# A feed forward block in float32: the first product by seven half-sized products, the second with half the tokens' sums held in PSUM

## The chip, the cores and the metric

The kernel runs on one core of one Trainium2 chip. The metric is the device time of one execution in microseconds (us), lower is better, here as the median of 3 runs. The core has five engines that run side by side and wait for each other by semaphores: TensorE (PE) multiplies, VectorE (DVE), ScalarE (ACT) and GpSimd (POOL) work on elements, and SyncE (SP) issues the transfers (DMA), in the order of its queue.

## The reference, cut to what matters

Two blocks are computed, one behind the other, on 1024 tokens of width 1024, all in float32. The change is in the last piece of the second block, which is

```
x = x + mix @ w_out_2                          # 1024 x 1024
h = rmsnorm(x, norm2_g_2)
x = x + square(relu(h @ w_up_2)) @ w_down_2    # 1024 -> 4096 -> 1024
return rmsnorm(x, final_g_2)
```

## The kernel before

A float32 operand is split into a high part that PE takes in its fast float32 form (F32R) and a rest: ACT copies the high part, DVE subtracts it (`split`, L248; `weights`, L252, the same). A product is then three matmuls (`mm3`, L242 to L246): high x high, high x rest, rest x high. PE adds them up in a PSUM bank of 128 x 512; there are eight banks.

Memory is laid out by hand in a few large tiles: `xa` and `xc` hold the split, transposed tokens (`xh`, `xl`) and the split weights (three slots each for high and rest, `rwh`, `rwl`), `fa` holds raw loads (`rraw`, two slots) and float32 data, and a phase tile (`self.ta`; t604a, t791a, t816a in the rows) is given out anew by `phase`. A slot is used in turn by a ring, so who writes a slot waits for the last reader of what lay there.

`block3` (L1965) does the last piece. `project` multiplies with `w_out_2` in four column groups, eight token tiles each. In the fourth group each finished tile gets its residual (L1980), its norm (square on ACT L469, the root on POOL L464, the scaling L1984 on DVE) and is transposed on PE and split (`flip`, L1374). Then the loop over f0 runs: for each pair of hidden columns f (128 wide) it loads a piece of `w_up_2`, forms the hidden values of all 1024 tokens (`gemm_t`, 2 x 24 matmuls), takes relu and square and splits them (L1999 to L2002), loads and splits a row block of `w_down_2` (L2006), and multiplies the pair with it for all eight token tiles, adding each result on DVE to x in SBUF (L2021, 256 times). The whole second block is emitted in one `tc.block(schedule_with_timeline_sim=True)`: the framework's scheduler chooses each engine's order, which then is fixed in the program. All transfers are in SP's queue.

Of the kernel before, what the change touches and what calls it, by code (L numbers as in the profile page):

```python
# [191 lines left out]
class Kernel:  # L192
    def __init__(self, tc, es, A):
        self.tc, self.nc, self.A = tc, tc.nc, A
        self.cst = self.pool(es, "cst", 1)
        self.sm = self.pool(es, "sm", 2)
        self.dr = self.pool(es, "dr", 1, space=DRAM)
        ap = self.pool(es, "ap", 1)
        pp = self.pool(es, "pp", 1, space=PSUM)
        self.xa = ap.tile([128, 22912], F32R, name="xa")  # L200
        self.fa = ap.tile([128, FO + FS], F32, name="fa")
        self.pa = pp.tile([128, 4096], F32, name="psum")
        self.uid = 0
# [4 lines left out]
        self.xc = self.pool(self.xes, "xc", 1).tile([128, 4096], F32R, name="xc")  # L208
        self.xr = [ring(self.xa, 8192 * g, 4096, 2) for g in range(2)] + [ring(self.xc, 0, 2048, 2)]
        self.rraw = ring(self.fa, 0, 1088, 2)  # L210
        self.rwh, self.rwl = ring(self.xa, 16384, 1088, 3, Slots), ring(self.xa, 19648, 1088, 3, Slots)
# [1296 lines left out]
    def conformer_out(self, ys):  # L1508
        nc, V = self.nc, self.nc.vector
        zr = ring(self.xa, 8192, 1024, 4)  # L1510
# [290 lines left out]
    def diff_attention(self, W, ys):  # L1801
# [16 lines left out]
        for i in range(len(seq) + LAG + 1):  # L1818
# [146 lines left out]
    def block3(self):  # L1965
        nc, V, A = self.nc, self.nc.vector, self.A
        self.tes.close()
        self.xes.close()
        self.phase(F32, TS + 4096)
        rx = self.F(0, 1024, 8)  # L1970
        rr = self.F(8192, 512, 2)
        self.rny = self.T(0, 1024, 3)
        g2 = self.T(3072, 1024, 1).get()
        nc.sync.dma_start(g2.ap, A["norm2_g_2"].broadcast_to([128, 1024]))
        self.pg, self.pt = self.banks(0, 1, 2, 3, 4), self.banks(5, 6, 7)
        x = [rx.get() for t in range(8)]
        for qd, _, t, p in self.project(A["w_out_2"][0], range(8), ks=K_OUT):
# [3 lines left out]
            if qd == 3:  # L1981
# [3 lines left out]
                self.flip(y, *self.xdst(t))  # L1985
        self.phase(F32R, TS + 4096)
        rhh, rhl = self.T(0, 1024, 4), self.T(4096, 1024, 4)
        rdh, rdl = self.T(8192, 1024, 3), self.T(11264, 1024, 3)
        G = 2
        for f0 in range(0, 32, G):  # L1990
            hs, ds = [], []
            for f in range(f0, f0 + G):
                w = self.weights([A["w_up_2"][0][:, f * 128:(f + 1) * 128]], 8, 128)
                hh, hl = rhh.get(), rhl.get()
                for g in range(2):
                    p = self.gemm_t(w, g, 512)
                    r = rr.get()
                    gs = slice(g * 512, g * 512 + 512)
                    nc.scalar.activation(r.ap, p.ap, AF.Relu)  # L1999
                    nc.scalar.activation(hh[:, gs], r.ap, AF.Square)  # L2000
                    V.tensor_tensor(r.ap, r.ap, r.ap, op=ALU.mult)
                    V.tensor_tensor(hl[:, gs], r.ap, hh[:, gs].bitcast(F32), op=ALU.subtract)  # L2002
                hs.append((hh, hl))
                self.done(w)
                rw = self.rraw.get([128, 1024])
                nc.sync.dma_start(rw.ap, A["w_down_2"][0][f * 128:(f + 1) * 128])  # L2006
                dh, dl = rdh.get(), rdl.get()
                self.split(dh.ap, dl.ap, rw.ap)
                ds.append((dh, dl))
            if f0 + G == 32:  # L2010
                fg = self.rraw.get([128, 1024])
                nc.sync.dma_start(fg.ap, A["final_g_2"].unsqueeze(0).broadcast_to([128, 1024]))
                self.rny = ring(self.xa, 0, 1024, 2)
            for t in range(8):
                ts = slice(t * 128, t * 128 + 128)
                for c in range(2):
                    cs = slice(c * 512, c * 512 + 512)
                    p = self.pg.get()
                    for i in range(G):
                        self.mm3(p.ap, hs[i][0][:, ts], hs[i][1][:, ts], ds[i][0][:, cs], ds[i][1][:, cs], i == 0, i == G - 1)  # L2020
                    V.tensor_tensor(x[t][:, cs], x[t][:, cs], p.ap, op=ALU.add)  # L2021
                if f0 + G == 32:
                    self.rms_row(x[t].ap, fg.ap)
                    nc.sync.dma_start(A["out"][t * 128:(t + 1) * 128], x[t].ap)
        self.tes.close()

    def run(self):
        self.mix = self.dr.tile([8, 128, NTOK], F32, name="mix")
        self.x1 = self.dr.tile([NTOK, 1024], F32, name="x1")
        self.x2 = self.dr.tile([NLAT, 1024], F32, name="x2")  # L2030
        self.x3 = self.dr.tile([NLAT, 1024], F32, name="x3")
# [43 lines left out]
```

## Time and profile before

| | us |
|---|---|
| median of 3 runs (2859.57 to 2865.55) | 2861.37 |
| the profiled execution, its time | 2860.13 |
| its span in the trace | 2858.4 |
| PE busy in it | 2705.8 (95%) |
| DVE, ACT, POOL busy | 1757.2, 1279.8, 594.0 |

Times in the rows count from the start of the span. A group of rows gives an instruction's line in the kernel, its engine, what it writes and reads, how often, and the mean length of one. A busy PE in these rows is PE with a matmul under way; its matmuls overlap, so the step from one start to the next tells the pace.

### The profile page before, as it was taken

How to read it: one execution, taken by the hardware profiler on the slowest of the kernel's cores; microseconds unless marked ns; L12 is line 12 of the kernel's file. 1: busy time of each engine (PE TensorE's matmuls, PEld its weight loads, DVE VectorE, ACT ScalarE, POOL GpSimd, SP SyncE). 2: the span in 40 equal slices, each digit the busy share in tenths (PEclk: the TensorE clock that was granted, in tenths of full speed). 3: DMA queues.
4: the chain of work that ended last, by engine and by line, in shares of the span. 5: the costliest groups of instructions: out<-in, count | busy, mean ns of one | idle time of the engine just before them, and what ended most of it. 6: DMA issues, size and time to landing. Idle time of an engine off the chain costs nothing. (4 is left out here: it accounts for less than half of the span.)

```text
span 2858.4 us, 43860 instructions
## 1 busy us (share of the span) xinstructions
PE 2705.8 (95%) x16606; PEld 2349.1 (82%) x16606; DVE 1757.2 (61%) x3684; ACT 1279.8 (45%) x2873; POOL 594.0 (21%) x760
## 2 busy tenths in 40 slices
PE   7999989999999999999998897899899999999998
PEld 3888879998889788888887786788798888888887
DVE  4788755546647787566364579788636444444445
ACT  4666545546526666456462332476523121121122
POOL 0122213413100122123130348265300000000000
PEclk9999999999999999999999999999999999999999
DMA  7001021212554111121135431432412111111111
GB/s 246 26 17 53 25 62 39 58 54 81 174 186 130 32 45 35 42 51 56 51 78 167 155 102 30 150 96 80 130 45 74 39 58 48 42 59 45 45 52 59
DMA packets 243616, 215.69 MB, mean 75 GB/s; under 512 B 14576, under 2 KB 222796, under 8 KB 243148
## 3 DMA queue, kind: packets, MB, share of 16 engines
q1 hardware_dynamic: 243404, 212.88, 24.5%
q8 instruction: 130, 2.13, 0.3%
q14 instruction: 82, 0.67, 0.1%
HBM read 178.39 MB, written 34.45 MB: 74 GB/s over the span
## 5 line engine op out<-in xcount | busy, mean ns | idle before, releaser
L244 PE MATMUL psum<-xa 128*128 128x256 f32 (+2 forms) x2992 | 1008.2, 338 | 8.9 <-ACT xa L265 1.9
L245 PE MATMUL psum<-xa 128*128 128x256 f32 (+2 forms) x2992 | 998.8, 334 | 5.9 <-POOL xa L266 3.7
L246 PE MATMUL psum<-xa 128*128 128x256 f32 (+2 forms) x2992 | 995.3, 333 | 2.9 <-POOL xa L266 2.2
L244 PEld LDWEIGHTS psum<-xa 128*128 128x128 f32 x2992 | 575.0, 193 | 61.3 <-ACT xa L265 2.9
L245 PEld LDWEIGHTS psum<-xa 128*128 128x128 f32 x2992 | 574.9, 192 | 55.2 <-POOL xa L266 3.9
L246 PEld LDWEIGHTS psum<-xa 128*128 128x128 f32 x2992 | 573.6, 192 | 51.2 <-POOL xa L266 2.8
L464 POOL TENSOR_TENSOR rsb<-rsa,half 128x1 f32<-128x1 f32 (+1 forms) x129 | 89.8, 696 | 1106.9 <-DVE rsa L462 1048.6
L266 DVE TENSOR_TENSOR xa<-fa,xa 128x1024 fp32r<-128x1024 f32 (+1 forms) x116 | 142.3, 1229 | 210.9 <-ACT xa L265 200.7
L265 ACT ACTIVATE xa<-fa 128x1024 fp32r<-128x1024 f32 (+1 forms) x136 | 143.8, 1059 | 283.1 <-PE psum L245 125.6
L2021 DVE TENSOR_TENSOR fa<-fa,psum 128x512 f32<-128x512 f32 x256 | 174.0, 686 | 126.9 <-PE psum L246 126.9
L805 POOL TENSOR_SCALAR fa<-fa,esk 128x640 f32<-128x640 f32 (+2 forms) x144 | 112.1, 791 | 449.6 <-DVE esk L803 342.9
L246 PE MATMUL psum<-t816a 128*128 128x512 f32 x512 | 199.5, 390 | 0.0
L245 PE MATMUL psum<-t816a 128*128 128x512 f32 x512 | 199.4, 389 | 0.0
L244 PE MATMUL psum<-t816a 128*128 128x512 f32 x512 | 199.3, 390 | 0.0
L249 ACT ACTIVATE t816a<-fa 128x1024 fp32r<-128x1024 f32 x32 | 34.0, 1061 | 358.7 <-PE psum L246 300.2
L1008 DVE SCALAR_TENSOR_TENSOR fa<-fa,vec 128x640 f32<-128x640 f32 (+2 forms) x128 | 110.4, 869 | 51.8 <-ACT fa L1006 43.3
L798 ACT ACTIVATE fa<-fa,nmx 128x640 f32<-128x640 f32 (+2 forms) x144 | 110.7, 769 | 34.8 <-DVE nmx L789 33.2
L789 DVE CUSTOM_DVE_ANT_0 fa<-psum,amask,nsink 128x640 f32<-128x640 f32 (+2 forms) x144 | 111.4, 773 | 21.1 <-PE psum L784 16.1
L246 PEld LDWEIGHTS psum<-t816a 128*128 128x128 f32 x512 | 96.1, 188 | 20.3
L245 PEld LDWEIGHTS psum<-t816a 128*128 128x128 f32 x512 | 96.1, 188 | 20.2
L244 PEld LDWEIGHTS psum<-t816a 128*128 128x128 f32 x512 | 96.1, 188 | 20.1
L1504 DVE SCALAR_TENSOR_TENSOR t604a<-t604a,cols 128x1024 f32<-128x1024 f32 x60 | 105.7, 1765 | 2.5 <-ACT t604a L1501 1.3
(472 smaller groups left out, 5148.3 us busy)
## 6 DMA issues: line engine op xcount, KB each, us to landing
fa<-in_w_in_dram SPq DMA_DIRECT2D x64, 512.0 KB
fa<-in_w_ada_dram SPq DMA_DIRECT2D x48, 512.0 KB
fa<-in_w_up_dram SPq DMA_DIRECT2D x32, 512.0 KB
fa<-in_w_down_dram SPq DMA_DIRECT2D x32, 512.0 KB
fa<-in_w_out_dram SPq DMA_DIRECT2D x24, 512.0 KB
fa<-in_w_in_dram SPq DMA_DIRECT2D x32, 256.0 KB
fa<-mix SPq DMA_DIRECT2D x18, 448.0 KB
x<-fa SPq DMA_DIRECT2D x62, 128.0 KB
```

The costliest lines, as they stand in the source:

```text
L244: mm(out, lh, rh, start=start, stop=False)
L245: mm(out, lh, rl, start=False, stop=False)
L246: mm(out, ll, rh, start=False, stop=stop)
L265: self.nc.scalar.activation(h.ap, r.ap, AF.Copy)
L266: (self.nc.gpsimd if self.wpool else self.nc.vector).tensor_tensor(l.ap, r.ap, h.ap.bitcast(F32), op=ALU.subtract)
L464: self.nc.gpsimd.tensor_tensor(r, e, self.half.broadcast_to([128, m]), op=ALU.pow)
L789: TTR = lambda o, i, m, init, acc: V.tensor_tensor_reduce(out=o, in0=i, in1=m, scale=-0.125, scalar=init, op0=ALU.add, op1=ALU.min, accum_ ...
L798: nc.scalar.activation(p[:, :nk], p[:, :nk], AF.Exp, scale=-1.0, bias=out, accum_out=sm[:, j:j + 1])
L805: nc.gpsimd.tensor_scalar(P[j][:, :nk], P[j][:, :nk], e[:, j:j + 1], 0.0, op0=ALU.mult, op1=ALU.add)
L1008: nc.vector.scalar_tensor_tensor(y, U[i][:, lo + tap:hi + tap], col(tap), y, op0=ALU.mult, op1=ALU.add)
L1504: self.nc.vector.scalar_tensor_tensor(y.ap, z[:, j:j + 1024], self.col("dw", 2 * j + i), y.ap, op0=ALU.mult, op1=ALU.add)
L2021: V.tensor_tensor(x[t][:, cs], x[t][:, cs], p.ap, op=ALU.add)
```

## The change

`w_up` is multiplied by Strassen's scheme. The 1024 tokens, the 1024 input channels and the 4096 hidden columns are cut in two halves each, and instead of eight products of half blocks there are seven (`UP`), each of a sum or difference of token blocks with a sum or difference of weight blocks. I call them product 0 to 6, and the eight column groups of 256 in each a unit: a unit has 24 matmuls of 128 x 512, so there are 56 units. The token blocks come from `z`, the transposed normalized tokens in float32 (ACT copies them from PSUM, L1990; no split there any more); POOL adds them (L2026) and they are split once for each product. A unit's weights are loaded (one or two pieces of 512 KB), added on POOL where there are two (L2042), and split. Each result goes to one or two of four accumulators: the first time by an ACT copy (L2076), later by a DVE addition (L2079). After its last contribution ACT takes relu and square in place (L2083, L2084) and SP stores it to `hd` in DRAM (L2085). `down` then takes half the tokens at a time: the sums of 512 tokens x 1024 columns stay in the eight banks over all 32 hidden groups, and hidden values and `w_down` are loaded and split for each pair of groups (L2100, L2106), `w_down` once for each half. The residual x goes by DRAM (`x4`) and comes back for one addition per bank. To make room, x stands in the phase tile until then, so its loads (L1978) move; tiles `xc` and a new `xg` are given back before the seven products.

```
-        self.xa = ap.tile([128, 22912], F32R, name="xa")
+        self.xa = ap.tile([128, 14720], F32R, name="xa")
...
+        self.xc, self.xg = xp.tile([128, 4096], F32R, name="xc"), xp.tile([128, 8192], F32R, name="xg")
+        self.xr = [ring(self.xa, 0, 4096, 2), ring(self.xg, 0, 4096, 2), ring(self.xc, 0, 2048, 2)]
...
     def block3(self):
...
-        self.phase(F32, TS + 4096)
-        rx = self.F(0, 1024, 8)
+        self.phase(F32)
+        rx, self.rny = self.T(0, 1024, 8), self.T(8192, 1024, 2)
+        z = self.F(0, 8192, 1).get([128, 8, NLAT])
...
+        self.z, self.rop, self.rtmp = z, ring(self.xa, 0, 2048, 4), self.rny
...
-                self.flip(y, *self.xdst(t))
-        for f0 in range(0, 32, G):
-            hs, ds = [], []
-            for f in range(f0, f0 + G):
-                w = self.weights([A["w_up_2"][0][:, f * 128:(f + 1) * 128]], 8, 128)
...
-            for t in range(8):
-                ts = slice(t * 128, t * 128 + 128)
+                nc.sync.dma_start(self.x4[t * 128:(t + 1) * 128], x[t].ap)
+                for i in range(2):
+                    tr = self.pt.get()
+                    for k in range(4):
+                        o = (4 * i + k) * 128
+                        nc.tensor.transpose(tr[:, k * 128:(k + 1) * 128], y[:, o:o + 128], self.ident)
+                    nc.scalar.activation(z[:, 4 * i:4 * i + 4, t * 128:(t + 1) * 128], tr.re("p (k n) -> p k n", k=4), AF.Copy)
+                if t == 6:
+                    first = list(self.up_tokens(0))[-1]
+        self.rraw.i = 0
+        raw = Ring(self.fa, [0, 1088], 1024)
+        ahead = [self.up_weights(0, 0, raw)]
+        self.tes.close()
+        self.xes.close()
+        self.phase(F32, TS + 12288)
+        raw.extend(self.T(18432, 1024, 4))
...
+    UP = [
+        ([(0, 0), (0, 1)], ALU.add, [(1, 1)], None, [((0, 0), -1), ((0, 1), 1)]),
+        ([(0, 0)], None, [(0, 1), (1, 1)], ALU.subtract, [((0, 1), 1), ((1, 1), 1)]),
+        ([(0, 0), (1, 1)], ALU.add, [(0, 0), (1, 1)], ALU.add, [((0, 0), 1), ((1, 1), 1)]),
+        ([(0, 1), (1, 1)], ALU.subtract, [(1, 0), (1, 1)], ALU.add, [((0, 0), 1)]),
+        ([(1, 1)], None, [(1, 0), (0, 0)], ALU.subtract, [((0, 0), 1), ((1, 0), 1)]),
+        ([(1, 0), (1, 1)], ALU.add, [(0, 0)], None, [((1, 0), 1), ((1, 1), -1)]),
+        ([(1, 0), (0, 0)], ALU.subtract, [(0, 0), (0, 1)], ALU.add, [((1, 1), 1)]),
+    ]
...
+    def up_tokens(self, m):
...
+            if op:
+                r = self.rtmp.get([128, 2, 512])
+                self.nc.gpsimd.tensor_tensor(r.ap, *src, op=op)
...
+    def up_weights(self, m, j, raw):
...
+        if op:
+            self.nc.gpsimd.tensor_tensor(rs[0].ap, rs[0].ap, rs[1].ap, op=op)
+        h, l = self.rwh.get([128, 4, 256]), self.rwl.get([128, 4, 256])
+        self.split(h.ap, l.ap, rs[0].ap)
...
+    def up(self, cur, raw, ahead):
...
+        cs = self.T(0, 512, 36, Slots)
...
+            for a in range(2):
+                p = self.pg.get()
+                for k in range(4):
+                    c = slice(a * 128, a * 128 + 128)
+                    self.mm3(p.ap, w[0][:, k, c], w[1][:, k, c], h[:, k], l[:, k], k == 0, k == 3)
+                f = 2 * j + a
+                for c, sign in self.UP[m][4]:
+                    if (c, f) not in acc:
+                        acc[c, f] = [cs.get(), left[c]]
+                        nc.scalar.activation(acc[c, f][0].ap, p.ap, AF.Copy, scale=float(sign))
+                    else:
+                        o = acc[c, f][0].ap
+                        V.tensor_tensor(o, o, p.ap, op=ALU.add if sign > 0 else ALU.subtract)
+                    acc[c, f][1] -= 1
+                    if not acc[c, f][1]:
+                        o = acc.pop((c, f))[0]
+                        nc.scalar.activation(o.ap, o.ap, AF.Relu)
+                        nc.scalar.activation(o.ap, o.ap, AF.Square)
+                        nc.sync.dma_start(self.hd[16 * c[1] + f, :, c[0] * 512:c[0] * 512 + 512], o.ap)
+                        cs.free(o)
...
+    def down(self, raw):
...
+        for t in range(2):
+            ps = [self.pg.get() for _ in range(8)]
+            last = []
+            for f in range(0, 32, 2):
+                o = operands(t, f)
+                if f >= 28 and t == 1:
+                    last.append(o)
+                    continue
+                for tt in range(4):
+                    for c in range(2):
+                        product(ps[2 * tt + c], o, tt, c)
```

What moves, at three places. The first is PE at the end of the last projection. Before, the products with `w_up` (128x512) begin while tiles are still being transposed (L1374):

```order
L1374 MATMUL psum<-ident,t791a 128x128 [waits DVE_49]
L1374 MATMUL psum<-ident,t791a 128x128 x3
L244 MATMUL psum<-xa 128x256
L245 MATMUL psum<-xa 128x256
L244 MATMUL psum<-xa 128x512 [waits Activation_49]
```

Now six tiles are transposed (L1989) ahead of the first 128x512 matmul, and POOL does the first half of product 0's token sum (L2026) ahead of the last two tiles' roots (L465), the second half behind them:

```order
L1989 MATMUL psum<-ident,t791a 128x128 [waits DVE_49,Activation_49]
L1989 MATMUL psum<-ident,t791a 128x128 x3
L1989 MATMUL psum<-ident,t791a 128x128 [waits Activation_49]
L1989 MATMUL psum<-ident,t791a 128x128 x3
L245 MATMUL psum<-xa 128x512 [waits Activation_49]
L245 MATMUL psum<-xa 128x512 x3
L1989 MATMUL psum<-ident,t791a 128x128 [waits DVE_49]
L1989 MATMUL psum<-ident,t791a 128x128 x7
L246 MATMUL psum<-xa 128x512 [waits DVE_49]
```

```order
L465 TENSOR_TENSOR rsb_20186<-rsa_20184,half 128x1 [waits DVE_49,Pool_49]
L2026 TENSOR_TENSOR t791a<-fa 128x1024 [waits DVE_49,DMAHW1_49,PE_49,Activation_49]
L465 TENSOR_TENSOR rsb_20230<-rsa_20228,half 128x1 [waits DVE_49,Pool_49]
L465 TENSOR_TENSOR rsb_20280<-rsa_20278,half 128x1 [waits DVE_49,Pool_49]
L2026 TENSOR_TENSOR t791a<-fa 128x1024 [waits PE_49]
L2042 TENSOR_TENSOR t816a<-t816a 128x1024 [waits DMAHW3_49,DMAHW4_49,DMAHW2_49,DMAHW5_49,DMAHW1_49,DMAHW6_49,DMAHW0_49,DMAHW7_49,DVE_49,PE_49]
```

The second is SP inside the feed forward part. Before, one piece of `w_up` and one of `w_down` for each f:

```order
L260 DMA fa<-in_w_up_dram 128x8x128 [waits DMAHW6_49,DVE_49]
L2006 DMA fa<-in_w_down_dram 128x1024 [waits DMAHW0_49,DVE_49]
L260 DMA fa<-in_w_up_dram 128x8x128 [waits DMAHW1_49,DVE_49]
L2006 DMA fa<-in_w_down_dram 128x1024 [waits DMAHW2_49,DVE_49]
L2006 DMA fa<-in_w_down_dram 128x1024 [waits DMAHW4_49,DVE_49]
```

Now, in product 1, loads of coming units wait for DVE or POOL to leave their slot, and the stores to `hd` stand between them; a store waits for ACT's square:

```order
L2038 DMA t816a<-in_w_up_dram 128x4x256 [waits DVE_49]
L2085 DMA hd<-t816a 128x512 [waits DMAHW7_49,Activation_49]
L2038 DMA t816a<-in_w_up_dram 128x4x256 [waits DVE_49]
L2038 DMA fa<-in_w_up_dram 128x4x256 [waits DVE_49]
L2085 DMA hd<-t816a 128x512 [waits DMAHW2_49,Activation_49]
L2085 DMA hd<-t816a 128x512 [waits DMAHW3_49,Activation_49]
L2038 DMA t816a<-in_w_up_dram 128x4x256 [waits DMAHW4_49,DMAHW0_49,Pool_49]
L2038 DMA t816a<-in_w_up_dram 128x4x256 [waits DMAHW5_49,DVE_49]
```

The third is SP at the end of the attention of the second block. Before, the loads of x (L1979) are spread between the attention's own transfers:

```order
L1593 DMA sgd<-fa 128x256 [waits DMAHW3_49,Activation_49]
L1979 DMA fa<-x_79 128x256 [waits DMAHW4_49,DMAHW2_49,DMAHW7_49,DMAHW0_49,Pool_49]
L1979 DMA fa<-x_79 128x256 [waits DMAHW5_49]
L1979 DMA fa<-x_79 128x256 [waits DMAHW6_49]
L1979 DMA fa<-x_79 128x256
L1593 DMA sgd<-fa 128x256 [waits Activation_49]
```

Now all 32 (L1978) stand behind the weights of `w_out` and wait for the last user of the attention's phase tile:

```order
L261 DMA fa<-in_w_out_dram 128x4x256 [waits DMAHW2_49,Pool_49]
L261 DMA fa<-in_w_out_dram 128x4x256 [waits DMAHW4_49,DVE_49]
L1972 DMA fa<-in_norm_g_dram 128x1024 [waits DVE_49,PE_49]
L1978 DMA t791a<-x_82 128x256 [waits DVE_49,PE_49,Pool_49]
L1978 DMA t791a<-x_82 128x256 x3
L1978 DMA t791a<-x_82 128x256 [waits DMAHW3_49]
```

The listed order also tells the count of 128 x 512 matmuls in the feed forward part: 3072 before (1536 and 1536), 2880 now (1344 and 1536).

## Rows read from the trace of the kernel before

**Rows 1.** The page: busy time of each engine, and POOL in 40 slices (tenths).
```profile
PE 2705.8 (95%) x16606; PEld 2349.1 (82%) x16606; DVE 1757.2 (61%) x3684; ACT 1279.8 (45%) x2873; POOL 594.0 (21%) x760
...
POOL 0122213413100122123130348265300000000000
```

**Rows 2.** Busy time by stretch, of the feed forward part (with the granted clock).
```profile
core 0: us, PE busy (x) PEld busy (x) DVE busy (x) ACT busy (x) POOL busy (x), PEclk, DMA share, GB/s
2200.00:2800.00 600.00, 600.00 (x2643) 495.70 (x2642) 284.40 (x384) 121.56 (x166) 0.00 (x0) 1.00 0.16 48
```

**Rows 3.** Instructions in order of time, PE, in the last product.
```profile
2842.15 0.39 PE L244 MATMUL psum<-t816a 128*128 128x512 f32 x1
...
2844.87 0.39 PE L244 MATMUL psum<-t816a 128*128 128x512 f32 x1
```

**Rows 4.** Instructions in order of time, DVE and SP, at the end.
```profile
2850.51 0.69 DVE L2021 TENSOR_TENSOR fa<-fa,psum 128x512 f32<-128x512 f32 x1 [0.17 <-PE psum L246]
...
2854.66 0.33 SPq L2024 DMA_DIRECT2D out_dram<-fa  x1
```

**Rows 5.** Groups by line and form, 2150 to 2858: count, busy us, mean ns.
```profile
L2021 DVE TENSOR_TENSOR fa<-fa,psum 128x512 f32<-128x512 f32 x256 | 174.0, 686 | 126.9 <-PE psum L246 126.9
...
L2000 ACT ACTIVATE t816a<-fa 128x512 fp32r<-128x512 f32 x64 | 40.5, 633 | 2.0
L250 DVE TENSOR_TENSOR t816a<-fa,t816a 128x1024 fp32r<-128x1024 f32 x32 | 39.1, 1222 | 68.1 <-ACT t816a L249 68.1
L1999 ACT ACTIVATE fa<-psum 128x512 f32<-128x512 f32 x64 | 37.4, 585 | 72.5 <-PE psum L246 70.7 <-DVE t816a L2002 1.9
...
L249 ACT ACTIVATE t816a<-fa 128x1024 fp32r<-128x1024 f32 x32 | 34.0, 1061 | 358.7 <-PE psum L246 300.2 <-DMA fa<-in_w_down_dram 58.5
```

**Rows 6.** The same by form for POOL, 1600 to 2030: its additions of 128x1024.
```profile
L266 POOL TENSOR_TENSOR xa<-fa,xa 128x1024 fp32r<-128x1024 f32 x20 | 51.7, 2587 | 182.2 <-ACT xa L265 180.7 <-DVE ne L1360 1.5
```

**Rows 7.** In order of time, POOL, then DVE, 1607 to 1620.
```profile
1611.17 2.40 POOL L266 TENSOR_TENSOR xa<-fa,xa 128x1024 fp32r<-128x1024 f32 x1 [100.73 <-ACT xa L265]
...
1617.49 2.40 POOL L1354 TENSOR_TENSOR t604a<-fa 128x1024 f32<-128x1024 f32 x1 [0.36 <-DVE ne L1358]
...
1607.97 0.41 DVE L1290 TENSOR_TENSOR fa<-fa 128x256 f32<-128x256 f32 x1
1611.46 2.38 DVE L1290 TENSOR_TENSOR fa<-fa 128x256 f32<-128x256 f32 x1 [3.08 <-DMA fa<-x]
...
1617.59 0.42 DVE L1289 TENSOR_TENSOR fa<-psum,fa 128x256 f32<-128x256 f32 x1
```

**Rows 8.** In order of time, SP and ACT, around one load of `w_down`.
```profile
2328.93 6.14 SPq L2006 DMA_DIRECT2D fa<-in_w_down_dram  x2
...
2332.38 1.06 ACT L249 ACTIVATE t816a<-fa 128x1024 fp32r<-128x1024 f32 x1 [4.93 <-DMA fa<-in_w_down_dram]
```

**Rows 9.** Busy time by stretch, columns as in rows 2.
```profile
18.00:22.00 4.00, 4.00 (x14) 1.33 (x13) 0.25 (x1) 0.00 (x0) 0.00 (x0) 1.00 1.05 340
1620.00:1640.00 20.00, 12.13 (x73) 10.68 (x71) 15.63 (x33) 17.23 (x28) 14.71 (x9) 0.80 0.46 157
```

**Rows 10.** In order of time, DVE and ACT: the last tile's norm, first relu.
```profile
2151.28 0.41 DVE L1980 TENSOR_TENSOR fa<-fa,psum 128x256 f32<-128x256 f32 x1
...
2152.33 1.05 ACT L469 ACTIVATE t791a<-fa 128x1024 f32<-128x1024 f32 x1
...
2154.38 1.28 DVE L1984 SCALAR_TENSOR_TENSOR t791a<-fa,rsb,t791a 128x1024 f32<-128x1024 f32 x1 [0.72 <-POOL rsb L464]
...
2155.03 0.60 ACT L1999 ACTIVATE fa<-psum 128x512 f32<-128x512 f32 x1 [0.43 <-PE psum L246]
```

**Rows 11.** By stretch (columns as in rows 2), then line L1902, then DVE in order of time.
```profile
2085.00:2120.00 35.00, 35.00 (x294) 35.00 (x294) 8.16 (x16) 2.12 (x2) 0.00 (x0) 1.00 0.10 31
...
L1902 PE MATMUL psum<-ident,t604a x8: 272/272/273, 2047.4 to 2066.3; 128*128 128x128 f32 x8
...
2056.22 0.28 DVE L1962 TENSOR_SCALAR t604a<-psum,drs 128x64 f32<-128x64 f32 x1 [4.77 <-PE psum L1955]
```

More of the change, by code (lines that the diff above doesn't have):

```diff
@@ L1509, in conformer_out @@
         nc, V = self.nc, self.nc.vector
-        zr = ring(self.xa, 8192, 1024, 4)
+        zr = ring(self.xg, 0, 1024, 4)
         zh, zl = [zr.get(), zr.get()], [zr.get(), zr.get()]
@@ new lines, in block3 @@
+        self.rraw.i = 0
[5 more added lines that the diff above has]
+        raw.extend(self.T(18432, 1024, 4))
+        self.rtmp = raw
+        self.up(first, raw, ahead)
+        self.down(raw)
+        self.tes.close()
+    UP = [
[7 more added lines that the diff above has]
+    ]
@@ new lines, in up_tokens @@
+    def up_tokens(self, m):
+        blocks, op = self.UP[m][:2]
+        h, l = self.rop.get([128, 4, 512]), self.rop.get([128, 4, 512])
+        yield h, l
+        for k in (0, 2):
+            src = [self.z[:, 4 * c + k:4 * c + k + 2, t * 512:t * 512 + 512] for t, c in blocks]
+            if op:
+                r = self.rtmp.get([128, 2, 512])
+                self.nc.gpsimd.tensor_tensor(r.ap, *src, op=op)
+                src = [r.ap]
+            self.split(h[:, k:k + 2], l[:, k:k + 2], src[0])
+            yield h, l
@@ new lines, in up_weights @@
+    def up_weights(self, m, j, raw):
+        blocks, op = self.UP[m][2:4]
+        rs = []
+        for k, n in blocks:
+            r = raw.get([128, 4, 256])
+            o = n * 2048 + j * 256
+            self.nc.sync.dma_start(
+                r.ap, self.A["w_up_2"][0][k * 512:k * 512 + 512, o:o + 256].rearrange("(k p) c -> p k c", p=128))
+            rs.append(r)
+        if op:
+            self.nc.gpsimd.tensor_tensor(rs[0].ap, rs[0].ap, rs[1].ap, op=op)
+        h, l = self.rwh.get([128, 4, 256]), self.rwl.get([128, 4, 256])
+        self.split(h.ap, l.ap, rs[0].ap)
+        return h, l
@@ new lines, in up @@
+    def up(self, cur, raw, ahead):
+        nc, V = self.nc, self.nc.vector
+        self.pg = self.banks(0, 1, 2, 3, 4, 5, 6, 7)
+        cs = self.T(0, 512, 36, Slots)
+        left = {}
+        for _, _, _, _, outs in self.UP:
+            for c, _ in outs:
+                left[c] = left.get(c, 0) + 1
+        acc = {}
+        units = [(m, j) for m in range(7) for j in range(8)]
+        nxt = None
+        for i, (m, j) in enumerate(units):
+            if i + 1 < len(units):
+                ahead.append(self.up_weights(*units[i + 1], raw))
+            if j == 0:
+                h, l = cur
+                nxt = self.up_tokens(m + 1) if m < 6 else None
+            if nxt and j in (2, 3, 4):
+                cur = next(nxt)
+            w = ahead.pop(0)
+            for a in range(2):
[18 more added lines that the diff above has]
+                        cs.free(o)
+            self.done([w])
```

85 lines of the change are left out of this document (43 added, 42 removed).

## The prediction

> **What bounds the kernel now.** I read the page first: PE is busy for 2705.8 of 2858.4 us, no other engine for more than 1757 [rows 1]. That is a mean over both blocks, so the stretch that is changed comes next, by the view of busy time by stretch: from 2200 to 2800 PE is busy 600.00 of 600 us with 2643 matmuls at granted clock 1.00, while DVE works 284.4, ACT 121.6 and POOL not at all, and the transfers take a share of 0.16 [rows 2]. Nothing but PE ends last there, so a matmul less is worth one step of PE. The step is read from starts, since matmuls overlap: 12 of 128x512 lie between the starts at 2842.15 and 2844.87, 2.72 us or 0.2267 each [rows 3]; 600 us over 2643 gives 0.2270. Last the end: the last addition starts at 2850.51, the last store is issued at 2854.66, and the span ends at 2858.4 [rows 4]. The changed kernel ends in the same way (the last products, one addition, norm, store), so I leave these 8 us as they are.
>
> **What is removed.** 3072 matmuls of 128x512 become 2880: 192 x 0.2267 = **43.5 us**. In this measure a unit (24 matmuls) lasts 5.44 us, a product (8 units) 43.5, the seven 304.7, `down` 348.2.
>
> **What is added beside PE.** It costs nothing as long as it fits under 5.44 us for each unit. Its prices are rows of the same sizes: a split of 128x1024 is 1.06 on ACT and 1.22 on DVE, an addition from PSUM 0.686 on DVE, a copy from PSUM 0.585 and a relu or square 0.633 on ACT [rows 5], an addition of 128x1024 on POOL 2.59 [rows 6]. ACT is fullest in products 1 and 4, where 16 results become final: 32 x 0.633 + 16 x 0.585 + 10 x 1.06 (eight weight splits, two of tokens) = 40.2 of 43.5 us. DVE is fullest in product 2, with four additions a unit: 4 x 0.686 + 1.22 + 2 x 1.22 / 8 = 4.27 of 5.44. POOL needs 2.59 in 40 of the 56 units.
>
> POOL and DVE disturb each other. While POOL's addition ran from 1611.17 to 1613.57, a DVE operation with both inputs in SBUF took 2.38 us instead of 0.41 and ended with it; one that read PSUM took 0.42 beside another such addition [rows 7]. So the accumulations, which read PSUM, should pass, and the split on DVE (1.22) can be held for up to 2.4. In product 2 this makes 4.27 + 2.4 = 6.67 us a unit at worst, 1.23 over, or 9.8 us in eight units.
>
> The transfers: products 1, 4 and 6 each load 16 x 512 KB and store 16 x 256 KB, 12.6 MB in 43.5 us or 289 GB/s. A stretch with the queues full moved 340 GB/s [rows 9]. It fits, with little to spare. `down` moves 1.5 MB in 10.9 us, 145 GB/s.
>
> **The loop that could set the pace** goes through the six slots for raw weights. Two for a unit, so a slot must come round in three units, 16.3 us. A lone load of 512 KB was issued at 2328.93 and used at 2332.38, 3.45 us later [rows 8]; at 340 GB/s the second piece adds 0.524 MB / 340 = 1.54 and a store's share 0.77; then POOL's 2.59, ACT's 1.06, DVE's 1.22: 10.6 us. This leaves 5.7 for waits in four queues that keep their order. They exist: SP's loads stand behind stores that wait for ACT's square, ACT's copies behind a slot of `cs` whose last store must have landed, the splits behind both. PE is covered by eight banks, four units of results. The trace has no such loop; its bounds are 0 (all waits within 5.7) and about 25 us (a unit 0.6 over in the 40 with an addition). I take **4**, near the lower end, because the sum of durations has a third of the loop to spare.
>
> **The start of the seven products.** Before, the first relu starts at 2155.03, 3.75 us after the last tile's residual at 2151.28, so PE was then already in `w_up`; there is no gap [rows 10]. Now product 0 needs a token sum in two halves of the channel pieces. Its tokens are tiles 0 to 3, long done, but in POOL's queue the second half stands behind the roots of the last two tiles, and so behind their norms. From the last residual to the scaling of that tile took 3.10 us, 2151.28 to 2154.38, so the root is there just before; then 2.59 of POOL, and a split of 1.06 and 1.22: second half ready 3.1 + 4.9 = about 8 us after the projection. PE has in that time, once the first half is split (I take 1 us after the projection, from its place one tile earlier), 24 matmuls of two units with the first two channel pieces, 5.44 us, and the 16 transposes of two tiles, 0.9 at a quarter of a 512-column matmul each: covered to 7.3. The rest is 0.7 at the second half and about 1 at the first, and each of the four hand-overs between engines takes some tenths (ACT's relu began 0.43 after an idle time that PE ended [rows 10]). Bounds are 0 and 8 (nothing of the 24 runs early). I take **2.5**.
>
> **Transitions.** From `up` to `down` and from one half of the tokens to the other, the first banks must be free and the first hidden values split. Those of half 0 are final from products 1 and 4, long before, and a bank's additions are over 9 us ahead of its next use. **1** us, between 0 and 3 (a load of 3.45 less its lead). In `down` the splits on ACT and DVE (one of hidden values and two of weights for each of 32 pairs) stand against 348 us of PE, each a pair (10.9 us) early: nothing; without that lead a pair would cost 2.3.
>
> **The loads of x** now wait for the end of the attention's phase tile. PE is busy 35.00 of 35 us with 294 matmuls in 2085 to 2120, 0.119 each, and the eight last transposes of the attention start between 2047.4 and 2066.3 [rows 11]. In the listed order 84 instead of 114 of the projection's matmuls stand ahead of them, 30 x 0.119 = 3.6 us of work less to fill waits with; but DVE waited 4.77 us there for PE [rows 11], so work ahead of the chain also delays it, and 27 matmuls (3.2 us) cover a load of 3.45 behind it. I take 0, between -1 and 3.6.
>
> **Sum**, against the profiled execution: 2860.1 - 43.5 + 4 + 2.5 + 1 = 2824.1. That execution lies 1.2 below the median of 2861.4, so about **2825**.
>
> **Does PE keep its clock?** From 1620 to 1640, where PE was busy 12.13 of 20 us, the granted clock was 0.80 [rows 9]; in the feed forward part it was 1.00 with no idle time [rows 2]. If short waits in each of the 40 units with an addition brought 0.80 there, a unit would last 5.44 / 0.80 = 6.80, and 40 x 1.36 = 54 us would be lost. [...]
>
> **The rivals.**
> (A) The forecast: PE stays the bound, everything added hides but some microseconds: 2817 (nothing lost, 2861.4 - 43.5 = 2817.9) to 2834.
> (B) Part of the stretches is set by another engine: DVE held by POOL in product 2 (+9.8) and short waits of the loop (up to 15): 2834 to 2852. For it: rows 7 show the hold, and ACT has 3 us to spare in products 1 and 4. Against it: eight banks even such stretches out.
> (C) The other side: the loop of raw slots sets the pace of all units with an addition. It decides from where its waits reach 8.7 us instead of 5.7: then the loop is 19.3, a unit 6.43, and 40 x 1.0 = 40 us eat the gain (with the 3.5 above). At 9.5 it is 20.15 us, a unit 6.72, 40 x 1.28 = 51: 2861.4 - 43.5 + 3.5 + 51 = 2872. For it: four ordered queues in one ring, and transfers at 289 of 340 GB/s. Against it: products 2 and 3 make no result final and store nothing, so that the loop is shorter there. Just short of the deciding point it ends between 2852 and 2867.
> (K) The clock, as above: 2861.4 - 43.5 + 7.5 + 54 = 2879. Against it: it needs a wait in nearly every unit first.
> That the change doesn't do what it says can be left out: 2880 matmuls are counted in the listed order.
>
> **How the numbers follow.** A .67, B .18, C just short of its point .04, C beyond it .08, K .03. A measurement here tells 0.2%, 5.7 us, from no change. Faster (below 2855.6): A, B and a part of C, .86; within 0.2% .03; slower .11. The range takes A and B, .85: from 2816 (nothing lost, and a microsecond won before the projection) to 2850.
>
> **What would show it.** In the stretches of `up`: PE busy nearly throughout, 0.227 us a matmul, clock 1.00. POOL's additions 2.4 to 2.6, DVE's split of weights somewhere between 1.2 and 3.6 while accumulations stay near 0.69. Transfers near 290 GB/s in products 1, 4 and 6. A gap of PE of some 2.5 us ahead of product 0, none between the halves of `down`. The forecast is wrong if PE's idle time ahead of `up`'s matmuls, put down to DVE's or ACT's splits of weights, adds up to more than 15 us (B), if it comes once in every unit of products 1 to 4 and 6 (C), or if the clock column falls below 1.00 in `up` (K); and if the last projection's matmuls wait for x, the loads of x were no free move.

## The result, and the profile after

The changed kernel takes 2835.7 us (median of 4 executions, 2834.1 to 2842.9) beside 2860.5 of the kernel before (4 executions): ratio 0.9916, 95% interval 0.9894 to 0.9939. It is 24.7 us faster; the forecast was 2825, 36 us faster. The profiled execution took 2835.9, its span is 2834.1.

The page of the changed kernel, the lines of [rows 1] and the granted clock in 40 slices:

```profile
PE 2666.5 (94%) x16414; PEld 2312.6 (82%) x16414; DVE 1723.9 (61%) x3530; ACT 1410.3 (50%) x3039; POOL 725.0 (26%) x810
...
POOL 0122203414200122123131149265501544200000
PEclk9999999999999999999999988999999999999999
```

PE has 192 matmuls less, 39 us less busy time and a smaller share of the span, so there are waits that were not there before. In POOL's row the slices 1 5 4 4 2 near the end, all 0 before, show its additions. The two slices of clock 8 lie ahead of the change. The view of PE's waits from 2000 on names two lines above all (waited for; us in total, times, longest):

```profile
PE psum L245 <- ACT xa L250: 5.8, 2, 3.8
PE psum L247 <- DVE xa L251: 4.6, 3, 2.6
```

L250 and L251 are the two halves of a split, on ACT and DVE. So PE waits for operands of its matmuls, five times by these two lines, and in none of them for a bank of results. The view by stretch (columns as in [rows 2]) shows the places: the start of product 0, a stall in product 2 and the time behind it, the time behind a stall in product 4, another stall there, and a stretch of `down`:

```profile
2160.00:2165.40 5.40, 5.40 (x21) 4.43 (x21) 3.51 (x2) 3.10 (x5) 2.91 (x2) 0.73 0.00 0
...
2263.40:2268.80 5.40, 2.79 (x13) 2.02 (x12) 5.36 (x5) 2.26 (x3) 4.02 (x2) 0.99 0.74 235
2268.80:2274.20 5.40, 5.40 (x18) 4.24 (x18) 5.40 (x8) 0.66 (x1) 1.74 (x1) 0.69 0.63 202
2274.20:2279.60 5.40, 5.40 (x25) 4.46 (x24) 4.40 (x7) 1.06 (x1) 1.45 (x2) 1.00 0.52 169
2361.30:2366.70 5.40, 5.40 (x19) 4.29 (x19) 3.87 (x6) 4.85 (x9) 2.19 (x1) 0.73 0.83 267
2377.60:2383.00 5.40, 3.91 (x18) 2.92 (x17) 3.82 (x3) 3.54 (x7) 4.80 (x2) 1.00 0.71 197
...
2500.00:2800.00 300.00, 300.00 (x1326) 248.47 (x1325) 109.93 (x101) 89.19 (x93) 2.21 (x4) 1.00 0.46 156
```

A stretch of 5.4 us at clock 1.00 holds 25 or 26 matmuls (those that reach over its edges counted too). Where PE idled for 2.6 us, it has 13, and in the next 5.4 us, with PE busy all the time, 18, at a clock of 0.69. So this idle time is paid nearly twice. In `down` there is none: 300.00 of 300 at 1.00, 1326 matmuls at 0.2262.

**A ledger by counted matmuls.** To compare kernels I count the matmuls of 128x512 in order of time and take from each one's start 0.22665 us for every matmul ahead of it; what this number grows by is lost time, idle or slow clock alike (the expectations call it lag). It gives three amounts: the start (this number at the 192nd matmul, the end of product 0, counted from the last residual addition of the projection), what the seven products lose behind it, and the transition to `down`. The whole stretch runs from that last residual to the start of the last matmul; it is the three amounts and 2879 steps of 0.22665. Units are numbered from 0 through all products: unit 19 is the fourth of product 2, units 35 and 38 are the fourth and the seventh of product 4.

| us | start | in `up` | transition | whole stretch |
|---|---|---|---|---|
| before | 1.2 | 0.7 (first half of its loop) | - | 698.8 |
| changed | 12.4 | 11.3 | 0.0 | 676.3 |

The three losses of `up` are 4.75 (unit 19), 4.87 (unit 35) and 1.65 (unit 38). With 43.5 taken off, 11.2 for the start and 11.3 in `up`, -21.0 is accounted for, of -22.5; the rest is before's slightly slower pace, 0.2270 in [rows 2] against 0.2265: its number grows by 1.5 behind the start, to the last matmul. The end is as it was: the last matmul starts at 2825.81, the last addition at 2826.23, 7.8 us ahead of the span's end (7.8 before, [rows 4]).

Rows in order of time around the start, POOL, ACT, DVE, PE (start, us, engine, line, and the idle time before it with what ended it):

```profile
2149.34 1.03 PE L1989 MATMUL psum<-ident,t791a 128*128 128x128 f32 x8
2149.54 0.42 DVE L1979 TENSOR_TENSOR t791a<-t791a,psum 128x256 f32<-128x256 f32 x1 [0.37 <-PE psum L247]
...
2151.09 5.64 DVE L251 TENSOR_TENSOR xa<-fa,xa 128x1024 fp32r<-128x1024 f32 x3
...
2153.16 2.50 POOL L2026 TENSOR_TENSOR t791a<-fa 128x1024 f32<-128x1024 f32 x1 [3.30 <-PE psum L1989]
...
2155.68 1.06 ACT L250 ACTIVATE xa<-t791a 128x1024 fp32r<-128x1024 f32 x1 [0.88 <-POOL t791a L2026]
2156.66 0.14 DVE L463 TENSOR_SCALAR rsa<-nss 128x1 f32<-128x1 f32 x1
...
2161.98 2.40 POOL L2026 TENSOR_TENSOR t791a<-fa 128x1024 f32<-128x1024 f32 x1
```

The first half of product 0's token sum begins 3.6 us after the last residual (2149.54), not at it: it writes one of the two slots in which the tiles' norms take turns, and POOL waits 3.30 us for PE to transpose the tile there. Three splits take DVE 5.64 us (3 x 1.22 = 3.7 alone), the last of them 3.37 while POOL adds, and the first step of the next tile's root (DVE L463) stands behind them. Only that last one is of weights, those of unit 1. The two ahead of it are of product 1's tokens, which need no sum and are not used before 2205: until product 1 begins, only four weight splits read `fa`, of units 0, 1, 6 and 7, and e22 below, without the one of unit 1, keeps two. Only 2156.79 brings the first 128x512 matmul, after 3.77 us of idle time, and the second half of the sum begins at 2161.98.

The stall in unit 19, same view, SP first, then POOL, DVE and PE:

```profile
2253.27 10.44 SPq L2085 DMA_DIRECT2D hd<-t816a  x3
2264.14 4.76 SPq L2038 DMA_DIRECT2D t816a<-in_w_up_dram  x3
...
2256.89 2.39 POOL L2042 TENSOR_TENSOR t816a<-t816a 128x1024 f32<-128x1024 f32 x1 [6.57 <-DMA hd<-t816a]
2259.36 2.39 POOL L2026 TENSOR_TENSOR t816a<-fa 128x1024 f32<-128x1024 f32 x1
2261.71 2.41 POOL L2042 TENSOR_TENSOR t816a<-t816a 128x1024 f32<-128x1024 f32 x1
2262.88 2.32 DVE L251 TENSOR_TENSOR xa<-t816a,xa 128x1024 fp32r<-128x1024 f32 x1 [5.80 <-ACT xa L250]
2264.06 3.36 POOL L2026 TENSOR_TENSOR fa<-fa 128x1024 f32<-128x1024 f32 x1
2266.32 2.19 DVE L251 TENSOR_TENSOR xa<-t816a,xa 128x1024 fp32r<-128x1024 f32 x1
2268.56 0.70 PE L247 MATMUL psum<-xa 128*128 128x512 f32 x1 [2.61 <-DVE xa L251]
```

POOL has two additions for weights (L2042) and, between and behind them, the two token sums of the next product (L2026), 10.5 us in one row without a gap. The token sums write raw slots too, so two of the six are not there for loads; and SP sends no load between 2253.27 and 2264.14, since three stores stand ahead. DVE's splits take 2.32 and 2.19 instead of 1.22, and PE gets its low parts of the weights (the rest, on DVE) 2.61 us late.

### The profile page after: what moved, and what is told of

It reads as the page before. It is cut to its first block, busy times and chain, and to the rows that moved or that the text cites. A ratio compares the mean times of both kernels' runs of the same rounds, so it can differ in the third digit from the quotient of the medians.

```text
span 2834.1 us, 44013 instructions
## 1 busy us (share of the span) xinstructions
PE 2666.5 (94%) x16414; PEld 2312.6 (82%) x16414; DVE 1723.9 (61%) x3530; ACT 1410.3 (50%) x3039; POOL 725.0 (26%) x810
## 5 line engine op out<-in xcount | busy, mean ns | idle before, releaser
L245 PE MATMUL psum<-xa 128*128 128x512 f32 (+2 forms) x2200 | 779.8, 356 | 13.4 <-ACT xa L250 6.7
L246 PE MATMUL psum<-xa 128*128 128x512 f32 (+2 forms) x2200 | 775.4, 353 | 4.3 <-POOL xa L267 3.0
L247 PE MATMUL psum<-xa 128*128 128x512 f32 (+2 forms) x2200 | 773.4, 352 | 5.4 <-DVE xa L251 4.6
L245 PEld LDWEIGHTS psum<-xa 128*128 128x128 f32 x2200 | 421.6, 192 | 68.6 <-ACT xa L250 7.7
L247 PEld LDWEIGHTS psum<-xa 128*128 128x128 f32 x2200 | 421.3, 191 | 58.8 <-DVE xa L251 6.6
L246 PEld LDWEIGHTS psum<-xa 128*128 128x128 f32 x2200 | 421.9, 192 | 56.5 <-POOL xa L267 3.2
L465 POOL TENSOR_TENSOR rsb<-rsa,half 128x1 f32<-128x1 f32 (+1 forms) x129 | 90.0, 698 | 780.8 <-DVE rsa L463 723.5
L245 PE MATMUL psum<-xa,xg 128*128 128x256 f32 (+1 forms) x864 | 248.8, 288 | 1.7 <-DVE fa L1523 1.1
L247 PE MATMUL psum<-xa,xg 128*128 128x256 f32 (+1 forms) x864 | 245.7, 284 | 0.0
L246 PE MATMUL psum<-xa,xg 128*128 128x256 f32 (+1 forms) x864 | 245.7, 284 | 0.0
L251 DVE TENSOR_TENSOR xa<-fa,xa 128x1024 fp32r<-128x1024 f32 (+2 forms) x121 | 139.2, 1162 | 165.3 <-ACT xa L250 165.1
L251 DVE TENSOR_TENSOR xa<-t816a,xa 128x1024 fp32r<-128x1024 f32 x84 | 115.1, 1372 | 175.5 <-ACT xa L250 171.9
L250 ACT ACTIVATE xa<-fa 128x1024 fp32r<-128x1024 f32 (+2 forms) x121 | 112.4, 942 | 171.5 <-PE psum L247 63.7
L267 DVE TENSOR_TENSOR xa<-fa,xa 128x1024 fp32r<-128x1024 f32 (+1 forms) x84 | 103.2, 1230 | 125.3 <-ACT xa L266 120.9
L250 ACT ACTIVATE xa<-t816a 128x1024 fp32r<-128x1024 f32 x84 | 88.3, 1054 | 167.4 <-PE psum L247 108.2
L245 PEld LDWEIGHTS psum<-xa,xg 128*128 128x128 f32 x864 | 163.9, 190 | 3.0 <-DVE fa L1523 1.5
L246 PEld LDWEIGHTS psum<-xa,xg 128*128 128x128 f32 x864 | 163.6, 189 | 0.7 <-issue 0.7
L247 PEld LDWEIGHTS psum<-xa,xg 128*128 128x128 f32 x864 | 163.5, 189 | 0.4 <-issue 0.3
L245 PE MATMUL psum<-xg,xa 128*128 128x512 f32 x376 | 154.1, 411 | 1.3 <-ACT xa L266 0.5
L247 PE MATMUL psum<-xg,xa 128*128 128x512 f32 x376 | 152.0, 405 | 2.7 <-POOL xa L267 2.7
```

Source lines behind the costliest of these rows:

```text
L245: mm(out, lh, rh, start=start, stop=False)
L246: mm(out, lh, rl, start=False, stop=False)
L247: mm(out, ll, rh, start=False, stop=stop)
L250: self.nc.scalar.activation(hi, src, AF.Copy)
L251: self.nc.vector.tensor_tensor(lo, src, hi.bitcast(F32), op=ALU.subtract)
L267: (self.nc.gpsimd if self.wpool else self.nc.vector).tensor_tensor(l.ap, r.ap, h.ap.bitcast(F32), op=ALU.subtract)
```

## The experiments

Two questions: what makes the stalls in `up`, and what makes the start. My theory T for the first: the token sums of the next product, by the slots that they take, by POOL's time, or both. Rival L: the loop of six raw slots is too long by its own waits, as in the forecast's case of short waits. For the second, first a theory S (the slots shared with the norms), then S2. The numbers of all runs stand in one table behind them. The framework's scheduler orders each kernel anew, so an edit can move other instructions too. Runs e1 to e16 have one time each, with the kernel before at 2872.1 beside e1 to e4 and at 2861.0 beside e11 to e16, so the ledger and not the whole time tells them apart.

**e1_sum_early.** The sum of product 0 is asked for earlier.

```
-                if t == 6:
+                if t == 3:
                     first = list(self.up_tokens(0))[-1]
```


> The token sum of product 0 is asked for behind tile 3 of the last projection instead of behind tile 6 (its tokens are tiles 0 to 3). Theory: the first 24 matmuls of product 0 start 3.8 us of idle time late and then at a low clock, because this sum stands in POOL's queue and in the two slots of y between the last tiles' norms; then the start gets 6 to 9 us shorter: 2827 to 2830. Rival: the last tiles' norms and transposes set the start anyway, or the sum's slots now hold up tiles 4 to 7 by as much: 2834 or more.

2850.0, start 23.5 us instead of 12.4: the rival, by more than it said. The sum now held both slots of the norms, so tiles 4 to 7 came through one behind the other, and PE waited at the end for weights whose slots the phase tile frees only behind the last norm (a wait of 5.54 for ACT's split at 2183.69).

**e2_no_token_sums.** Leaves out the sums of products 2, 3, 5 and 6.

```
-            if op:
+            if op and m == 0:
                 r = self.rtmp.get([128, 2, 512])
```


> Leaves out the token additions of products 2, 3, 5 and 6 (one block of tokens is split in place of the sum); the weight additions, loads and matmuls stay. Theory T (the two token additions of a product, between weight additions on POOL and in the same six raw slots, set off the stalls in units 19, 35 and 38): these stalls, 11.3 us of lag with the low clock behind them, go: about 2824.5. Rival L (the loop of the six raw slots is too long by its own waits for stores and queues): the stalls stay or move, 2831 or more.

In `up` 0.0 us are lost, with all 40 weight additions, loads and stores in place: T, and L falls for six slots. PE's waits from 2060 to the end have no line for DVE's L251 on operands of `up` any more:

```profile
PE psum L245 <- ACT xa L250: 6.3, 3, 3.8
PE psum L1989 <- DVE t791a L1983: 0.9, 1, 0.9
```

The time, 2831.0, is 6 above the expectation: 1.9 us came back at the transition, the start is 0.9 longer, and this execution reached the last residual at 2152.8, 3.3 later than the changed kernel's, in a part that is the same in both.

**e3_own_slot.** The same sums, in a slot of their own.

```
-        self.rtmp = raw
+        self.rtmp = self.F(8192, 1024, 1)
```


> The token sums of products 2, 3, 5 and 6 get a slot of their own (the norm's weights lay there), so they take none of the six raw slots; POOL does the same additions. If it is the slots that they take (T, by slots): the lag of 11.3 us in up falls below 3, about 2825 to 2828. If it is POOL's time, four additions of 2.4 to 3.4 one behind the other (T, by POOL), or the loop itself (L): 8 us or more of the lag stay, 2832 to 2836.

The loss in `up` falls from 11.3 to 2.4 us (most of it at unit 35), as T by slots says; but the transition now loses 7.3, and the time stays at 2835.8. PE's row there:

```profile
2475.49 2.93 PE L245 MATMUL psum<-xa 128*128 128x512 f32 x6 [4.90 <-ACT xa L250]
```

**e4_four_slots.** Four raw slots instead of six.

```
-        raw.extend(self.T(18432, 1024, 4))
+        raw.extend(self.T(18432, 1024, 2))
```


> Four raw slots instead of six: a slot must come round in two units, 10.9 us, instead of 16.3. The sum of durations of the loop was 10.6. If the waits in the loop are small outside the three stalls (theory T): units of products with additions grow by 0 to 1 us, 2845 to 2875. If the loop is nearly full with its waits, 16 us (rival L): 8 us a unit, 40 x 2.6 more, 2920 to 2945.

2855.5, 25.0 us lost in `up` and 4.7 at the transition. So 13.7 more in 40 units, 0.3 each, and the token sums, which now take two of four slots, may have a part in it: a loop of 10.9 us is nearly enough. The sum of durations (10.6) was about right, and ordinary waits in the loop are small.

**e11_sum_in_x.** The two sums of product 0 lie where tiles 0 and 1 of x lay.

```
-        self.z, self.rop, self.rtmp = z, ring(self.xa, 0, 2048, 4), self.rny
+        self.z, self.rop, self.rtmp = z, ring(self.xa, 0, 2048, 4), self.T(0, 1024, 2)
```


> Only the place of the two partial sums of product 0 changes: they lie where tiles 0 and 1 of x lay (stored to DRAM by then) and no longer in the two slots in which the tiles' norms take turns. Theory S (the shared slots tie the sums and the last two norms to one another): from the last residual of the projection to the steady pace of product 0 the time falls from 12.4 us to 4 to 7, so the kernel gets 5 to 8 us shorter, about 2829. Rival (the splits of the first weights ahead of them on ACT and DVE, and the length of the chain through tile 7, set it): 10 us or more, 2834 or more.

2849.3; the start takes 17.1. S in this form falls. Both sums now run ahead of the last two tiles' roots on POOL, so the order has changed with the slots, and PE waits in another place, for a transposition whose tile is normed late:

```profile
PE psum L1989 <- DVE rsa L463: 7.0, 1, 7.0
PE psum L247 <- DVE xa L251: 6.7, 4, 3.5
```

**e12_own_slot_shift.** e3 with the ring turned on by two.

```
-        self.rtmp = raw
+        self.rtmp = self.F(8192, 1024, 1)
...
+        raw.i += 2
         self.down(raw)
```


> Own slot for the token sums of products 2, 3, 5 and 6 as before, and the ring of raw slots turned on by two ahead of the last part, so that its first loads meet the same slots as in the changed kernel. If the 7.3 us lost at the transition with the own slot came from that meeting: they fall to 0 to 2, 2827 to 2830. If it is SP's order or the late stores: 5 or more stay, 2834. In up 2.4 us of lag stay either way.

Transition 0.0, 2.2 us in `up`, 2833.7. The loss of e3 was the meeting of the two rings that share two slots (the raw weights' six and the two of `rraw`, which `down` uses for hidden values): 96 loads leave the ring of six at its first slot, 96 and eight token sums at its third. It is not the only cause of a loss there: e15, below, leaves it at the third slot and loses 2.3.

**e15_spread.** The sums of the next product three units apart.

```
-            if nxt and j in (2, 3, 4):
+            if nxt and j in (0, 3, 6):
```


> The two token sums of the next product are asked for three units apart (column groups 3 and 6 instead of 3 and 4), still in the six raw slots. If a stall needs both sums close together (two of six slots and 5 us of POOL at once): the lag in up falls from 11.3 to 0 to 5, 2825 to 2830. If one sum is enough to empty the ring: 8 or more, 2833 or more.

2837.2. In `up` 5.9 us are lost, half, now in units 19, 22 and 25, and 2.3 at the transition. Between the two cases: a sum alone can still bring a short stall.

**e16_both.** e11 and e12 together.
```
+        self.z, self.rop, self.rtmp = z, ring(self.xa, 0, 2048, 4), self.T(0, 1024, 2)
...
+        self.rtmp = self.F(8192, 1024, 1)
...
+        raw.i += 2
```


> The other place for the sums of product 0, the own slot for the later sums and the turn of the ring together. If the parts add up by theories S and T: lag 5 to 7 less at the start and 9 to 11 less in up, 2818 to 2823. If one removed wait only uncovers another: 2828 or more.

2827.0, but by its upstream part: the whole stretch is 671.0, longer than e12's. `up` loses 0.9, the start 17.5 as in e11.

The start stayed open, so S2: DVE's queue sets it, with POOL's hold on DVE. Three kernels on top of e12, timed in three rounds.

**e18_sum_dve.**

```
-                self.nc.gpsimd.tensor_tensor(r.ap, *src, op=op)
+                (self.nc.gpsimd if m else self.nc.vector).tensor_tensor(r.ap, *src, op=op)
```


> On top of the own slot and the turned ring: the two partial sums of product 0 are added on DVE instead of POOL, still in the slots that the norms use. Theory S2 (the start is set by DVE's queue: splits of weights and tokens that POOL's sums hold, 5.6 to 6.1 us for three instead of 3.7, ahead of the norms of the last tiles, and by POOL's sums standing between the roots): from the last residual to the steady pace 7 to 9 us instead of 12.4, kernel 2822 to 2825. Rival (the two shared slots are the tie, on whatever engine the sum is): 11 to 13 us, 2827 to 2830.

2832.2, ratio 0.9886 (0.9871 to 0.9901); start 13.8. The three splits ahead of the norms on DVE do take less, as S2 says:

```profile
2151.97 3.49 DVE L251 TENSOR_TENSOR xa<-fa,xa 128x1024 fp32r<-128x1024 f32 x3
```

The two sums (1.22 each) are then DVE's own work, so its queue is relieved little, and the start is no shorter: 13.8 beside 13.5 and 12.5 in two executions of the same kernel with the sums on POOL (e12, e24), a little over the rival's 11 to 13.

**e19_sum_dve_x.** As e18, with the sums where x lay (the line of e11).

> As the kernel with the sums of product 0 on DVE, and these sums where tiles 0 and 1 of x lay. With slots alone and POOL the start took 17.5 us. By S2 (POOL's hold on DVE made that): 5 to 8 us, kernel 2820 to 2824. By the rival (a free slot lets the sums stand ahead of the norms, which costs on any engine): 13 us or more, 2828 or more.

2834.4, ratio 0.9894 (0.9877 to 0.9910); start 17.2. The rival's time again: without POOL's hold the start is as long as with it (e16: 17.5), so that part of S2 falls. But it is another start. Rows in order of time, ACT, PE, SP, PE; the last residual is at 2147.59:

```profile
2148.74 1.05 ACT L250 ACTIVATE xa<-t791a 128x1024 fp32r<-128x1024 f32 x1
2149.84 1.22 PE L245 MATMUL psum<-xa 128*128 128x512 f32 x4 [2.45 <-ACT xa L250]
...
2167.76 2.03 SPq L2039 DMA_DIRECT2D t816a<-in_w_up_dram  x4
...
2173.22 0.80 PE L245 MATMUL psum<-xa 128*128 128x512 f32 x1 [5.54 <-ACT xa L250]
```

The first half is split 1.2 us after the last residual, and units 0 and 1 run. Then PE waits 5.54 us for the weights of unit 2. Their slots lie in the new phase tile, so their loads go out only when the old one is free, at 2167.76: PE's order has the last four transpositions (2167.09) behind all 48 matmuls of units 0 and 1, though DVE had scaled that tile by 2158.72.

**e22_one_early.** One slot filled ahead of the phase tile's end.

```
-        raw = Ring(self.fa, [0, 1088], 1024)
+        raw = Ring(self.fa, [0], 1024)
...
         raw.extend(self.T(18432, 1024, 4))
+        raw.extend(Ring(self.fa, [1088], 1024))
```


> On top of the own slot and the turned ring, sums of product 0 on POOL as in the changed kernel: only one slot for w_up is filled ahead of the phase tile's end instead of two, so that one split of weights less stands on DVE among the last norms. By S2: DVE's hold shrinks by 2, but unit 1 of product 0 must wait for a load behind the last norm: 10 to 14 us to the steady pace, kernel 2826 to 2830. If the weights' splits play no part: over 14, as much later as the load.

2838.2, ratio 0.9899 (0.9883 to 0.9914); start 18.5. The row of DVE that had three splits:

```profile
2156.05 2.35 DVE L251 TENSOR_TENSOR xa<-fa,xa 128x1024 fp32r<-128x1024 f32 x2
```

The split that is gone saves nothing: the first matmul comes 7.25 us after the last residual, as in the changed kernel (7.26). The load behind the last norm costs 2.77 us of PE's time at 2175.49. The two splits of product 1's tokens stand ahead of the last norms in every one of these kernels; none moves them.

**e24_own_slot_timed.** The kernel of e12 in five rounds.

> The kernel with the own slot for the token sums of products 2, 3, 5 and 6 and the turned ring, timed. Its one execution ran from the last residual to the last matmul in 668.2 us, the changed kernel's in 676.3. If this holds, it is 8 us faster than the changed kernel: ratio to the kernel before 0.988 to 0.990 (the changed kernel 0.9916). If the 8 us are scatter of single executions: 0.991 to 0.993.

2830.3, ratio 0.9880 (0.9862 to 0.9899), whole stretch 668.9. In both single executions of this kernel the stretch is 7 to 8 us shorter than in the changed kernel; the intervals of the two ratios (0.9894 to 0.9939 there) still touch. The expected 0.988 to 0.990 holds. It has the lowest ratio that the runs show, 35 us (1.2%) ahead of the kernel before in the same rounds, though e18's 0.9886 is within its interval.

| us, one profiled execution each | start | in `up` | transition | whole stretch |
|---|---|---|---|---|
| e1 sum early | 23.5 | 11.6 | 0.0 | 687.6 |
| e2 no token sums | 13.3 | 0.0 | 1.9 | 667.7 |
| e3 own slot | 12.9 | 2.4 | 7.3 | 675.1 |
| e4 four slots | 13.6 | 25.0 | 4.7 | 695.8 |
| e11 sum in x | 17.1 | 11.7 | 0.0 | 681.4 |
| e12 own slot, ring turned | 13.5 | 2.2 | 0.0 | 668.2 |
| e15 spread | 13.4 | 5.9 | 2.3 | 674.2 |
| e16 both | 17.5 | 0.9 | 0.0 | 671.0 |
| e18 sum on DVE | 13.8 | 3.3 | 0.0 | 669.6 |
| e19 sum on DVE, in x | 17.2 | 3.0 | 0.0 | 672.8 |
| e22 one slot early | 18.5 | 2.7 | 0.0 | 673.8 |
| e24 as e12 | 12.5 | 3.9 | 0.0 | 668.9 |

## Why the prediction was right, and where it was short

**What is removed** was right: 43.5 us. From the end of product 4 on, 1920 matmuls, the ledger grows by 0.03 us, and `down` runs at 1.00 without a gap. PE stayed the bound outside of the stalls, and the time fell within the range, 11 us above the forecast, at the seam of rivals A (to 2834) and B (from 2834). With the measured terms the sum closes: 2860.1 - 43.5 + 11.2 (start) + 11.3 (`up`) - 1.5 (before's slower pace) - 1.7 (the last residual comes earlier) = 2835.9, as measured. The two amounts taken off at the end were not forecast; without them the miss would be 3 us larger, so that much of the nearness is luck.

**The start** was the larger miss: 2.5 forecast, bounds 0 to 8, 11.2 measured (12.4 less before's 1.2). The step that failed: "once the first half is split (I take 1 us after the projection, from its place one tile earlier)". Its split on ACT began 6.1 us after the last residual, because its slot waits for the transposition of a tile. And the start pays a slow clock, 0.73 from 2160 to 2165.4, which the term had not. The 16 transposes, put at 0.9 in all, a quarter of a 128x512 matmul each, step by 0.107 us where the granted clock is 1.00 (eight from 2166.28, in 2165.4 to 2170.8), nearly half of 0.2267: 1.7 in all. Also, before, ten matmuls of the loop had already run when the last residual began; now none.

That step is not the only bound. In e19 it came out as forecast (1.2 us), and the start still took 17.2, since the weights of unit 2 wait for the end of the old phase tile, a wait that the term left out. In the changed kernel the same split of unit 2 begins at 2171.25, 21.7 us after the last residual, and without loss PE would ask for it after about 10.9 (48 steps). So taking the first wait away need not shorten the start. What would shorten the start stays open. Sums asked for earlier, in other slots or with a weight split less ahead of them made it 4 to 11 us longer, and on DVE it was the same within the scatter: S fell in the form tested, and of S2 the part on POOL's hold. I argue from e18 that norms, splits and sums together load ACT, DVE and POOL in these 15 us, and that an order which serves one holds up another. Kernels with the splits of product 1's tokens behind the norms, with slots for unit 2 outside the phase tile, or with a first product that needs no token sum were not tried.

**The loop of raw slots** was sized at 4, and `up` lost 11.3. Its price of 10.6 us a turn held (e4). The term missed that the token sums of products 2, 3, 5 and 6 draw on the same ring: I had put them at nothing but POOL's and DVE's time. With them away nothing is lost (e2); with a slot of their own 1 to 4 us are (e3, e12, e24, and e16 with 0.9). So the mechanism of case B was right, short waits in a few units, but its trigger was the token sums; stores, loads and queues by themselves cost nothing in e2. What part of the 1 to 4 is POOL's time, the runs do not separate.

**POOL's hold on DVE** was as in [rows 7]: splits of weights took 2.2 to 2.3 in the stall, accumulations from PSUM 0.68 on the mean and 0.69 at most. The 9.8 us of product 2 did not come: in e2, with POOL's additions for weights in place, product 2 loses nothing.

**The transition** was 1 and is 0. That it can be 7.3 when the rings meet otherwise was not among the bounds (0 to 3).

**The loads of x** were put at 0. The last residual came at 2149.5, and at 2151.3 in the kernel before, but in e16 at 2146.0 and in e11 at 2157.9, with the same code up to there, so nothing can be read from it.

**The clock (K)** did not fall throughout, but it fell behind three waits, to 0.73, 0.69 and 0.73 in the stretches shown. The forecast had named a clock below 1.00 in `up` as a sign that it is wrong; this sign came, although the time stayed in the range. In units 19 and 35 the price of the waits, with this fall behind them, was nearly doubled (4.75 us for 2.61, 4.87 for 2.57), and no term had it. The other sign, PE's idle time ahead of `up` over 15 us, did not come: 5.8 + 4.6 = 10.4. In product 2, behind the 2.61 us, rows of PE in order of time:

```profile
2268.56 0.70 PE L247 MATMUL psum<-xa 128*128 128x512 f32 x1 [2.61 <-DVE xa L251]
2269.06 0.63 PE L245 MATMUL psum<-xa 128*128 128x512 f32 x1
2269.48 0.63 PE L246 MATMUL psum<-xa 128*128 128x512 f32 x1
...
2272.31 0.39 PE L247 MATMUL psum<-xa 128*128 128x512 f32 x1
2272.54 0.40 PE L245 MATMUL psum<-xa 128*128 128x512 f32 x1
```

The steps are 0.42 and then 0.23 us; the granted clock was 0.69 from 2268.8 to 2274.2 and 1.00 in the next 5.4 us. The idle time of 2.61 cost 4.75 in all, and in unit 35 waits of 2.05 and 0.52 cost 4.87; in unit 38 a wait of 1.49 cost 1.65, little more than itself, and the clock from 2377.6 to 2383.0 was 1.00.

**Transfers** were forecast at 289 GB/s for products 1, 4 and 6. They moved 219, 216 and 311 (2205.5 to 2249.0, 2340.8 to 2390.8, 2434.3 to 2477.9): product 6 has the loads of `down` on top. From 2400 to 2450, in products 5 and 6, it was 294.

## What to carry to other kernels

Count every user of a ring of buffers, the rare ones too: two extra requests in a turn of six slots stalled PE, while a third fewer slots cost ordinary turns little. To price a rescheduled start, ask for every input of its first units, not only the first, when its slot comes free: with one wait gone (e19) the next one set the time. A wait of PE can cost more than its length, here 4.75 us for 2.61. Two rings over the same memory have a phase, which moves when a request is added or removed.

## What was not expected of the hardware

The kernels e11 and e16 are the same up to the projection's last residual, and yet it came at 2157.9 in one execution and at 2146.0 in the other. The mean granted clock of the whole execution was 0.976 in the first and 0.982 in the second; this goes the same way, but that it makes the whole difference is not shown. Two executions of one kernel (e12, e24) differ there by 3.2 us and in the whole stretch behind it by 0.7. A single time of a kernel thus tells less than its own stretch.
